# Two scan directions in lockstep, and one modulation product moved from VectorE to TensorE

## The chip, the cores and the metric

The kernel runs on one core of a Trainium2 chip. The metric is device time in microseconds for one execution of the whole program, and the median over several runs is compared. The profile is one further execution.

## The reference

A backbone of two layers over 1024 latent tokens of width 1024, with a prefix of 256 context tokens. Layer 0 mixes tokens with RWKV-7 scans in two directions, layer 1 with Fourier transforms; each is followed by a squared-ReLU MLP. Shift, scale and gate of every sub-layer come from a product of SiLU(c) with `mod_w`. Cut to what matters here:

```python
sh1, sc1, ga1, sh2, sc2, ga2 = jnp.split((silu_c @ mod_w[i] + mod_b[i])[:, None, :], N_MOD, axis=-1)
...
def step(s, inp):
    w_t, k_t, v_t, a_t, b_t = inp[:5]
    sa = jnp.einsum('bhvk,bhk->bhv', s, a_t)
    s = s * w_t[:, :, None, :] + sa[..., None] * b_t[:, :, None, :] + v_t[..., None] * k_t[:, :, None, :]
    y = jnp.einsum('bhvk,bhk->bhv', s, inp[5]) if with_out else None
...
for d in range(N_DIRS):
    rev = d == 1
    yc, s_ctx = _wkv_scan(st_c.get('r'), vh_c, *st_c['dirs'][d], s0, rev)
    yl, _ = _wkv_scan(st_l['r'], vh_l, *st_l['dirs'][d], s_ctx, rev)
    y_lat.append(yl)
```

There are 16 heads of 64 channels. The state of a head is a 64 by 64 matrix, and the latent scan starts from the state that the context scan of the same direction leaves.

## The kernel before

**Order of work.** Every operation is entered in a plan with an engine, a planned duration, the data it reads and writes, and for TensorE a load. `Plan.emit` then writes out an order for each engine: at each turn it takes the operation that can start first by its own model of times, and among equals the one with the longest tail of work behind it. On the chip each engine works through its list strictly in that order, and waits where data isn't there. The model also guesses the TensorE clock from planned loads, and puts dummy products on the identity matrix (L1814) where TensorE would otherwise stand still. A `flex` operation can go to one of several engines; the plan chooses.

**Stages.** `projections` computes keys, values, decays and so on and writes the scan's factors to DRAM. `scan` then takes 20 steps of 64 tokens: four of context (i = 0 to 3), sixteen latent. `rest` reads the scan's outputs back, gates and projects them, and runs the first MLP, the Fourier layer and the second MLP with products split in three.

**One scan step** (`scan_step`) handles 64 tokens of both directions d = 0, 1. Channels lie in eight tiles of 128, each of two heads (hh = 0, 1).

- Loads on SP: `bk` (512 KB a direction) and the `a`, `r` rows into `L`, later the values into `sv`.
- Scores: four TensorE operations (L945) into PSUM, spread by ScalarE (L954, L958) into `mab` and by VectorE, masked, into `L` (L961) and `l2` (L966).
- `bk` is turned by TensorE (L975, one operation of 16 transposes a direction, 64 rows by 128 columns of the array each) and copied to `bkt` (L979).
- `scan_invert` inverts the triangular blocks of both directions at once: transposes and small recursive products on VectorE (L1094 to L1138), then two TensorE operations on 32*32 tiles of the array, `h_mm` (L1145) and `t_mm` (L1156), 64 products each.
- The state that comes in is multiplied by the decay: two passes of 64 rows on VectorE into `sv` (L1001), one of 128 rows on GpSimd into `st` (L1004).
- For each direction in turn, a chain: `x_mm` (L1019), a ScalarE copy of half the rows (L1026), `u_mm` (L1031, 32*32 tiles), two ScalarE copies to `sv` (L1036), `o_mm` (L1044, 32*32 tiles), copy, `u_mm`, copies, then `s_mm` (L1056) and the new state (L1062). In latent steps `y_mm` (L1072, L1076) makes the output, which is copied (L1082) and stored.

A product of fp32 operands leaves two TensorE records in the trace, a transpose one. `sv` has a ring of three tiles, which the two directions take in turn.

**Modulation in the scan.** The first layer's four vectors that are needed after the scan (`mod_w[0][:, 2D:]`) are made beside it. `k_mwt` holds the weights transposed. From step 3 on, each of sixteen steps loads four pieces of 128 by 512 (L885, 256 KB each, ring `mw` of four), and VectorE multiplies each with a row of SiLU(c) and sums along it (L886). `mod_sum` adds the halves and the bias. The second layer's vectors are made in the same way during the first MLP (`modvecs`).

Of the kernel before, what the change touches and what calls it, by code (L numbers as in the profile page):

```python
# [12 lines left out]
AF = mybir.ActivationFunctionType  # L13
ALU = mybir.AluOpType
# [66 lines left out]
class Plan:  # L81
# [245 lines left out]
class Kernel:  # L327
# [449 lines left out]
    def factor(self, kt, low, d, c, k, k_k, kk, kkk, rr):  # L777
# [37 lines left out]
        self.flex_tt(n, bk[:, :ng, 0], gv(ta), p1[:, :ng], ALU.mult, [kta, kp1], [(kbk, 0)])  # L815
# [19 lines left out]
    def scan(self):  # L835
# [10 lines left out]
        for j, hp in enumerate(R["hp"]):  # L846
            plan.add("dve", 0.6, lambda hp=hp: nc.vector.tensor_copy(hp, self.cst[:, 0:32].rearrange("p (e c) -> p e c", e=1).broadcast_to(
                [P, 16, 32])), [self.kcst], [("hp", j)])
        self.state = {}
        for i in range(NCH):  # L850
            self.plan.step = i
            self.scan_step(i)
            if i == 3:
                past = plan.gate([("indt", 0), ("rts", 0), ("rts", 1)])
            if i in (3, 11):
                w, kw = slot("mw")
                self.silu_row(i // 8, lambda w=w: w, kw, [past, self.at])
            if 3 <= i < 19:
                for j in range(4):
                    w, kw = slot("mw")  # L860
                    self.mod_part(0, 16 + (i - 3) % 8 * 4 + j, (i - 3) // 8, lambda w=w: w, kw, [self.at])
            if i >= 11 and i < 19:
                self.mod_sum(0, 16 + (i - 11) * 4)
# [16 lines left out]
    def mod_part(self, layer, j, h, w, kw, after=()):  # L880

        nc = self.nc
        row = (j - 16 if layer == 0 else 32 + j) * P
        src = self.i["k_mwt"][row : row + P, h * 512 : h * 512 + 512]
        self.plan.add("q", 0.8, lambda: nc.sync.dma_start(w(), src), (), [kw], after=after, hold=0.7)  # L885
        self.plan.add("dve", 0.76, lambda: nc.vector.scalar_tensor_tensor(  # L886
            w(), w(), 1.0, self.silr, ALU.mult, ALU.mult,
            accum_out=self.macc[:, layer, h, j : j + 1]), ["silr"], [kw, ("macc", layer, h, j)])
# [11 lines left out]
    def scan_step(self, i):  # L900
# [3 lines left out]
        R0 = [slice(hh * 64, hh * 64 + 32) for hh in range(2)]  # L904
        R1 = [slice(hh * 64 + 32, hh * 64 + 64) for hh in range(2)]
# [24 lines left out]
        for d in range(2):  # L930
# [5 lines left out]
            for h4 in range(2):  # L936
# [13 lines left out]
                for hh, B in enumerate(BB):  # L950
# [3 lines left out]
                    plan.add("act", 0.38, lambda B=B, hh=hh, ys=ys: nc.scalar.activation(  # L954
                        mab[R0[hh], :, ys].rearrange("p w q t -> p q w t"),
                        B.tile[R0[hh]].rearrange("p (q w t) -> p q w t", q=4, w=4)[:, :, 0:2], AF.Copy, scale=-0.5),
                        [B], [(kM, d, hh, h4, 0)], B)
                    plan.add("act", 0.28, lambda bv=bv, hh=hh, ys=ys: nc.scalar.activation(  # L958
                        mab[R1[hh], 0, ys], bv()[R1[hh], :, 32:C], AF.Copy, scale=-0.5),
# [10 lines left out]
            BB = [self.plan.bank(range(4)) for _ in range(2)]  # L970

            def trs(BB=BB, bk=bk):
                for q in range(8):
                    for hh, rs in enumerate(HR):
                        nc.tensor.transpose(BB[hh].tile[:, q * C : (q + 1) * C], bk[rs, q, :], self.ident[rs, rs])  # L975

            plan.add("pe", 1.1, trs, [kb], [*BB, (kt_, 0), (kt_, 1)], load=0.5)
            for hh, B in enumerate(BB):
                plan.add("act", 0.68, lambda B=B, bkt=bkt, hh=hh: nc.scalar.activation(  # L979
                    bkt[:, hh].rearrange("p x t -> p (x t)"), B.tile, AF.Copy, scale=self.sgn[:, hh : hh + 1]),  # L980
                    [B, self.ksgn], [(kt_, hh)], B)
        tt, kT = self.scan_invert(mab, kM)

        for d in range(2):
# [12 lines left out]
            else:  # L997
                t, kt0, pcs = self.state[d]
                for hh in range(2):
                    rs = HR[hh]  # L1000
                    plan.add(("dve", "dve")[hh], 0.78, lambda rs=rs, hh=hh, d=d, t=t, sv=sv: (nc.vector, nc.vector)[hh].tensor_tensor(  # L1001
                        sv[rs, hh], t[rs], self.pcs[rs, d, :, i - 1 : i].broadcast_to([64, 8, C]), ALU.mult),
                        [kt0, *pcs], [(kv, "s0", hh), (kv, "s1", hh)])
                plan.add("pool", 1.22, lambda d=d, t=t, st=st: nc.gpsimd.tensor_tensor(  # L1004
                    st, t, self.pcs[:, d, :, i - 1 : i].broadcast_to([P, 8, C]), ALU.mult), [kt0, *pcs], [ks])
        for d in range(2):
            E = S[d]
            L, kL, sv, kv = E["L"], E["kL"], E["sv"], E["kv"]
            lall = [(kL, "a", 0), (kL, "a", 1)] + [(kL, "k", hh, h4) for hh in range(2) for h4 in range(2)]
            vall = [(kv, z, hh) for z in ("s0", "s1", "v") for hh in range(2)]  # L1010

            B, U = self.plan.bank(range(5,8)), self.plan.bank(range(5,8))
            quarter = [[slice(64 * z + 32 * hh, 64 * z + 32 * hh + 32) for hh in range(2)] for z in range(2)]

            def x_mm(B=B, L=L, sv=sv):
                for q in range(8):
                    for z in range(2):
                        for hh in range(2):
                            nc.tensor.matmul(B.tile[quarter[z][hh], q * C : (q + 1) * C], L[hh][:, q, 32 * z : 32 * z + 32],  # L1019
                                             sv[:, hh, q, :], start=z == 0 or q == 0, stop=z == 0)  # L1020

            self.at = plan.add("pe", 1.1, x_mm, lall + vall, [(B, 0), (B, 1)], B, load=0.78)
            for z, rows in enumerate((R0, R1)):
                half = slice(64 * z, 64 * z + 64)
                xs, kx = slot("xs")
                plan.add("act", 0.58, lambda B=B, xs=xs, half=half: nc.scalar.copy(xs[half], B.tile[half]), [(B, z)], [kx], B)  # L1026

                def u_mm(xs=xs, rows=rows, d=d, U=U, at=quarter[z]):
                    for q in range(8):
                        for hh in range(2):  # L1030
                            nc.tensor.matmul(U.tile[rows[hh], q * C : (q + 1) * C], tt[at[hh], d * 8 + q, :],  # L1031
                                             xs[at[hh], q * C : (q + 1) * C], start=True, stop=True)

                plan.add("pe", 1.08, u_mm, [kx, kT], [(U, z)], U, load=0.4)
                for hh in range(2):
                    plan.add("act", 0.58, lambda sv=sv, hh=hh, rows=rows, U=U: nc.scalar.copy(  # L1036
                        sv[rows[hh], hh].rearrange("p q c -> p (q c)"), U.tile[rows[hh]]), [(U, z)], [(kv, f"s{z}", hh)], U)
                if z:
                    continue

                def o_mm(B=B, sv=sv, d=d):
                    for q in range(8):
                        for hh in range(2):
                            nc.tensor.matmul(B.tile[quarter[1][hh], q * C : (q + 1) * C], mab[R0[hh], 1, d * 8 + q, :],  # L1044
                                             sv[R0[hh], hh, q, :], start=False, stop=q == 7)

                plan.add("pe", 1.08, o_mm, [(kv, "s0", 0), (kv, "s0", 1)] + [(kM, d, hh, h4, 0) for hh in range(2) for h4 in range(2)],
                         [(B, 1)], B, load=0.4)
# [15 lines left out]
            if lat:  # L1064
# [4 lines left out]
                def y_mm(B=Y, L=L, l2=l2, sv=sv, st=E["st"]):  # L1069
                    for q in range(8):  # L1070
                        for hh in range(2):
                            nc.tensor.matmul(B.tile[HR[hh], q * C : (q + 1) * C], L[hh][HR[hh], q, C:], st[HR[hh], q, :],  # L1072
                                             start=q == 0, stop=False)
                    for q in range(8):
                        for hh in range(2):
# [3 lines left out]
                plan.add("pe", 2.1, y_mm, vall + [E["ks"], (kL, "a", 0), (kL, "a", 1)]  # L1079
                         + [(k2, hh, h4) for hh in range(2) for h4 in range(2)], [Y], Y, load=0.85)  # L1080
# [5 lines left out]
    def scan_invert(self, mab, kM):  # L1086
# [23 lines left out]
        plan.add("dve", 1.5, four, [km], [kx, kta])  # L1110

        def double(n):

            for o in range(0, 16, 2 * n):
# [4 lines left out]
                def mul(o=o, ta=ta, pa=pa, z=z):  # L1119
                    p = at(ta, 0, [(n * n, n), (n, n), (1, n)])  # L1120
                    nc.vector.tensor_tensor(p, at(m, o + z, [(16, n), (0, n), (1, n)]), at(x, o, [(0, n), (1, n), (16, n)]), ALU.mult)
                    nc.vector.tensor_reduce(at(pa, 0, [(n, n), (1, n)]), p, AX.X, ALU.add)
                    nc.vector.tensor_tensor(p, at(x, o + z + n, [(16, n), (0, n), (1, n)]), at(pa, 0, [(0, n), (1, n), (n, n)]), ALU.mult)
                    nc.vector.tensor_reduce(at(x, o + z, [(16, n), (1, n)]), p, AX.X, ALU.add)

# [800 lines left out]
```

## Time and profile before

| what | value |
|---|---|
| median of 3 runs | 3099.05 us (3092.76 to 3102.13) |
| the profiled execution, its own time | 3100.86 us |
| span of the profile | 3099.1 us |
| mean granted TensorE clock | 0.93 |
| clock from 600 to 700 us, 1000 to 1100 us, 1600 to 1800 us | 0.71, 0.76, 1.00 |
| VectorE busy from 600 to 1300 us | 448.71 of 700 us |

Times in the profile are microseconds from the first instruction, single instructions are in ns where a row says so. A row of the timeline gives the start, the length from the first start to the last end, engine, line and operation, output and inputs, the tile of the array ("32*32": rows and columns used), and the count. A tile's letters stand for its place: `ps` for PSUM, the rest for places in SBUF. "issue" means that the engine waited for nothing that the profile shows. The granted clock is a share of full speed.

### The profile page before, as it was taken

Reading aid. Unit: us, or ns where it says so; the run is one execution under the profiler, and the core shown is the slowest. Engines: PE = TensorE matmul, PEld = TensorE weight load, DVE = VectorE, ACT = ScalarE, POOL = GpSimd, SP = SyncE. Lnnn points to the kernel's source line nnn. Section 1 sums busy time; section 2 is a strip of 40 time slices with the busy share of each in tenths; the row PEclk is TensorE's granted clock in tenths of the full one; section 3 lists DMA queues with packets and bytes.
Section 4 is the critical chain, followed back from the end, with each engine's and each line's share of the span. In section 5 each row is a group of like instructions: output and inputs, shape, how many; then the busy total and the mean of one; then the engine's idle time right before and its main releaser. Section 6 shows DMA issues by size and latency. Waiting matters only on the chain.

```text
span 3099.1 us, 65486 instructions
## 1 busy us (share of the span) xinstructions
PE 2905.6 (94%) x27884; PEld 2258.6 (73%) x27884; DVE 1902.2 (61%) x3316; ACT 998.6 (32%) x1943; POOL 535.9 (17%) x449
## 2 busy tenths in 40 slices
PE   9999989988878888799999999999899999999998
PEld 5443446477777777789878888888798788888887
DVE  5397785457666666687566556545877544554456
ACT  4363554245444555443211211111322111111121
POOL 2163452201001000111111001100331110111010
PEclk9999999967777877799999999999989999999999
DMA  9266476623344444553132323211031111111111
GB/s 276 86 182 174 136 194 177 160 66 100 107 128 124 134 117 120 158 186 102 58 109 92 96 89 107 70 48 47 8 120 42 52 47 38 55 48 48 41 45 55
DMA packets 297299, 313.03 MB, mean 101 GB/s; under 512 B 81024, under 2 KB 212224, under 8 KB 297008
## 3 DMA queue, kind: packets, MB, share of 16 engines
q1 hardware_dynamic: 295648, 304.01, 33.1%
q8 instruction: 219, 3.59, 0.5%
q0 software_dynamic: 1360, 4.84, 0.5%
q14 instruction: 72, 0.59, 0.1%
HBM read 246.38 MB, written 62.39 MB: 100 GB/s over the span
## 4 chain that ended last, share of the span: by engine, by line
PE 71%; DVE 10%; DMA 6%; issue 3%; ACT 2%; POOL 0%; SPq 0%; DVEq 0%; ACTq 0%; POOLq 0%
PE ps L364 16%; PE ps L366 16%; PE ps L365 16%; PE ps L617 4%; DMA sW<-in_k_mwt_dram 3%; PE ps L620 3%; PE ps L1031 2%; PE ps L945 2%; PE ps L1056 1%; PE ps L1044 1%; PE ps L1019 1%; PE ps L1072 1%; PE ps L1076 1%; DVE bU L456 1%; PE ps L1156 1%
## 5 line engine op out<-in xcount | busy, mean ns | idle before, releaser
L364 PE MATMUL ps<-rU,rU 128*128 128x512 f32 (+3 forms) x2632 | 979.0, 372 | 9.8 <-DVE rX L1509 8.0
L366 PE MATMUL ps<-rU,rU 128*128 128x512 f32 (+3 forms) x2632 | 974.9, 370 | 6.5 <-DVE rU L1239 3.7
L365 PE MATMUL ps<-rU,rU 128*128 128x512 f32 (+3 forms) x2632 | 974.6, 370 | 0.0
L364 PEld LDWEIGHTS ps<-rU,rU 128*128 128x128 f32 x2632 | 500.5, 190 | 105.1 <-DVE rX L1509 9.1
L366 PEld LDWEIGHTS ps<-rU,rU 128*128 128x128 f32 x2632 | 500.6, 190 | 98.0 <-DVE rU L1239 5.2
L365 PEld LDWEIGHTS ps<-rU,rU 128*128 128x128 f32 x2632 | 500.6, 190 | 89.5
L1509 DVE SCALAR_TENSOR_TENSOR rX<-ps,mods,rX 128x512 f32<-128x512 f32 (+1 forms) x528 | 375.6, 730 | 122.3 <-PE ps L366 120.5
L1239 POOL TENSOR_TENSOR rU<-rW,rU 128x512 fp32r<-128x512 f32 x73 | 117.2, 1611 | 1018.8 <-PE ps L366 521.7
L1488 ACT ACTIVATE rS<-ps 128x512 f32<-128x512 f32 x122 | 73.1, 599 | 680.9 <-PE ps L366 680.2
L620 PE MATMUL ps<-bU,bU 128*128 128x512 f32 (+1 forms) x544 | 237.5, 573 | 2.6 <-ACT bS L423 1.9
L423 ACT CAST rU<-rW 128x512 fp32r<-128x512 f32 x160 | 96.3, 616 | 346.8 <-PE ps L366 251.3
L423 DVE CAST rU<-rW 128x512 fp32r<-128x512 f32 x116 | 56.8, 500 | 221.0 <-PE ps L365 210.1
L423 DVE CAST rU<-rS 128x512 fp32r<-128x512 f32 (+1 forms) x99 | 46.9, 479 | 229.5 <-ACT rS L1491 203.4
L1239 DVE TENSOR_TENSOR rU<-rW,rU 128x512 fp32r<-128x512 f32 x201 | 175.5, 893 | 19.7 <-ACT rU L423 19.3
L620 PEld LDWEIGHTS ps<-bU,bU 128*128 128x128 f32 x544 | 100.2, 193 | 109.1 <-issue 98.2
L617 PE MATMUL ps<-bU,bU 128*128 128x512 f32 x304 | 141.7, 607 | 0.0
L945 PE MATMUL ps<-sU,sX 64*128 64x128 f32 (+1 forms) x1280 | 125.5, 353 | 16.8 <-DVE sU L961 7.8
L945 PEld LDWEIGHTS ps<-sU,sX 64*128 64x128 f32 x1280 | 111.9, 255 | 25.2 <-issue 11.7
L961 DVE TENSOR_TENSOR sU<-ps,sW 64x256 f32<-64x256 f32 x160 | 67.5, 422 | 85.7 <-ACT sX L954 44.8
L1239 POOL TENSOR_TENSOR rU<-rS,rU 128x512 fp32r<-128x512 f32 x39 | 60.7, 1559 | 280.8 <-ACT rU L423 125.9
L1036 ACT COPY sU<-ps 32x512 f32<-32x512 f32 x160 | 92.3, 577 | 43.4 <-PE ps L1031 40.2
L617 PEld LDWEIGHTS ps<-bU,bU 128*128 128x128 f32 x304 | 56.6, 192 | 61.6 <-issue 57.8
(268 smaller groups left out, 3899.2 us busy)
## 6 DMA issues: line engine op xcount, KB each, us to landing
rW<-in_mlp_w_dram SPq DMA_DIRECT2D x256, 256.0 KB
rW<-in_k_mwt_dram SPq DMA_DIRECT2D x96, 256.0 KB
sX<-s_bk SPq DMA_DIRECT2D x40, 512.0 KB
s_ar<-bU SPq DMA_DIRECT2D x32, 512.0 KB
sU<-s_ar SPq DMA_DIRECT2D x64, 256.0 KB
sW<-in_k_mwt_dram SPq DMA_DIRECT2D x64, 256.0 KB
bU<-in_rk_wk_dram SPq DMA_DIRECT2D x48, 256.0 KB
bU<-in_rk_wv_dram SPq DMA_DIRECT2D x48, 256.0 KB
```

The source lines that it names most:

```text
L364: nc.tensor.matmul(out, w[0], x[0], start=start, stop=False)
L365: nc.tensor.matmul(out, w[0], x[1], start=False, stop=False)
L366: nc.tensor.matmul(out, w[1], x[0], start=False, stop=stop)
L423: self.nc.scalar.copy(out, src) if e == "act" else self.engines[e].tensor_copy(out, src)
L617: fn = lambda B=B, x=x, w=w, ms=ms, kt=kt: nc.tensor.matmul(B.tile, x[:, ms], w, start=kt == 0, stop=kt == KT - 1)
L620: fn = lambda B=B, x=x, w=w, ms=ms, kt=kt, n=n: nc.tensor.matmul(B.tile[:, :n], w[:, ms], x[:, :n], start=kt == 0, stop=kt == KT - 1)
L945: nc.tensor.matmul(BB[hh].tile[:, j * P : j * P + nr], bk[HR[hh], q, :], L[hh][HR[hh], q, :nr], start=True, stop=True)
L961: plan.add("dve", 0.41, lambda bv=bv, ro=ro, hh=hh, q4=q4, d=d, L=L: nc.vector.tensor_tensor(L[hh][ro, q4, 0:C], bv()[ro, :, 0:C], self.ma ...
L1036: plan.add("act", 0.58, lambda sv=sv, hh=hh, rows=rows, U=U: nc.scalar.copy(sv[rows[hh], hh].rearrange("p q c -> p (q c)"), U.tile[rows[hh ...
L1239: plan.flex({"dve": n / 960 + 0.07, "pool": n / 440 + 0.08}, lambda e: self.engines[e].tensor_tensor(out(1), src(), f32(out(0)), ALU.subtr ...
L1488: plan.flex({"act": 0.53, "dve": 0.6}, lambda e, B=B, s=s: nc.scalar.activation(s.tile[:, :512], B.tile, AF.Relu) if e == "act" else nc.ve ...
L1509: plan.add("dve", n / 960 + 0.12, lambda B=B, m=m, n=n, xs=xs: nc.vector.scalar_tensor_tensor(xs(), B.tile[:, :n], self.mod(layer, 5, m), ...
```

## The change

The diff does several things, all in the scan:

- The two directions share `u_mm` and `o_mm`. The rows of a direction's two halves are swapped for d = 1 (`RZ`), so that four 32*32 tiles of the array serve both directions and both heads in one operation. `x_mm` writes both directions' results into two shared banks, one copy of 128 rows takes the place of two of 64, and the eight copies to `sv` may go to ScalarE or VectorE.
- The transposes of `bk` leave their own operation and are issued inside `h_mm` (direction 0) and `t_mm` (direction 1): after the four products of each y, one transpose. Each of the two is planned as two halves.
- The decay of the state is one VectorE pass of 128 rows into `st`, copied from there to `sv`; GpSimd has no part in it.
- `y_mm` is planned as two operations, `r_mm` and `y_mm`.
- The inversion's VectorE steps are planned one by one, and two of them read and write their scratch tile in another order.
- Modulation of the first layer: `k_mw1` holds the weights in their own order. `mod_block` loads four pieces a step, multiplies each on TensorE with a 32-column tile of SiLU(c) (one strip of the array each), copies the bank to SBUF on ScalarE, turns it with four products against `sel`, and copies eight columns out on VectorE. The rows of SiLU(c) (`silu_row`) are no longer made in the scan.

The core of the diff:

```diff
+                for q in range(8):
+                    for d, hh in four:
+                        rs = RZ[z][d][hh]
+                        nc.tensor.matmul(U.tile[rs, q * C : (q + 1) * C], tt[rs, d * 8 + q, :], xs[rs, q * C : (q + 1) * C],
+                                         start=True, stop=True)
...
+                plan.add("dve", 0.76, lambda d=d, t=t, st=st: nc.vector.tensor_tensor(
+                    st, t, self.pcs[:, d, :, i - 1 : i].broadcast_to([P, 8, C]), ALU.mult), [kt0, *pcs], [ks])
                 for hh in range(2):
-                    rs = HR[hh]
-                    plan.add(("dve", "dve")[hh], 0.78, ...
-                plan.add("pool", 1.22, ...
+                    plan.flex({"act": 0.58, "dve": 0.45}, lambda e, hh=hh, sv=sv, st=st: self.copy_on(e, sv[HR[hh], hh], st[HR[hh]]),
...
+        def turn(d, y):
+            nc.tensor.transpose(TB[d][y % 2].tile[:, y // 2 * C : (y // 2 + 1) * C], S[d]["bk"][HR[y % 2], y // 2, :], self.ident[HR[y % 2], HR[y % 2]])
...
-        def h_mm():
-            for y in range(16):
+        def h_mm(w):
+            for y in range(8 * w, 8 * w + 8):
                 for q in Q:
                     nc.tensor.matmul(H.tile[q, y * 16 : y * 16 + 16], mab[q, 0, y, :], xt[q, y, 0:16], start=True, stop=True)
+                turn(0, y)
...
+        def t_mm(w):
+            for y in range(8 * w, 8 * w + 8):
+                for q in Q:
+                    nc.tensor.matmul(T.tile[q, y * 32 : y * 32 + 32], hp[q, y, :], xd[q, y, :], start=True, stop=True)
+                turn(1, y)
...
+    def mod_block(self, j, h):
+        W = [slot("mw") for _ in range(4)]
+        for k, (w, kw) in enumerate(W):
+            ...
+            plan.add("q", 0.8, lambda w=w, src=src: nc.sync.dma_start(w, src), (), [kw], after=[self.at], hold=0.7)
+        def products():
+            for k, (w, _) in enumerate(W):
+                nc.tensor.matmul(B.tile[32 * k : 32 * k + 32], silc[:, 4 * h + k], w, start=True, stop=True)
+        plan.add("pe", 0.6, products, [kw for _, kw in W] + [ksil], [B], B)
+        plan.add("act", 0.58, lambda: nc.scalar.copy(e, B.tile), [B], [ke], B)
+        def turn():
+            for x in range(4):
+                nc.tensor.matmul(V.tile[:, 2 * x : 2 * x + 2], e[:, x * P : (x + 1) * P], self.sel, start=True, stop=True)
+        plan.add("pe", 0.5, turn, [ke], [V], V, load=0.0)
```

The planned durations in these lines are the scheduler's, not measurements. The rest of the kernel is built as before, in the order that the plan then gives.

More of the change, by code (lines that the diff above doesn't have):

```diff
@@ L903, in scan_step @@
         nr = P if lat else C
[L904 to L905 removed]
+        RZ = [[[slice(hh * 64 + 32 * (d ^ z), hh * 64 + 32 * (d ^ z) + 32) for hh in range(2)] for d in range(2)] for z in range(2)]
         HR = [slice(hh * 64, hh * 64 + 64) for hh in range(2)]
@@ L969, in scan_step @@
                             [B, self.kmask], [(k2, hh, h4)], B)
[L970 to L982, printed above, removed]
+        tt, kT = self.scan_invert(mab, kM, S)
         for d in range(2):
@@ L1018, in x_mm @@
                         for hh in range(2):
-                            nc.tensor.matmul(B.tile[quarter[z][hh], q * C : (q + 1) * C], L[hh][:, q, 32 * z : 32 * z + 32],
+                            nc.tensor.matmul(XB[z].tile[RZ[z][d][hh], q * C : (q + 1) * C], L[hh][:, q, 32 * z : 32 * z + 32],
                                              sv[:, hh, q, :], start=z == 0 or q == 0, stop=z == 0)
[L1022 to L1048, printed above, removed]
@@ L1049, in scan_step @@
+        for d in range(2):
+            E = S[d]
+            L, kL, sv, kv, vall = E["L"], E["kL"], E["sv"], E["kv"], vkeys[d]
             if i < NCH - 1:
@@ L1150, in scan_invert @@
             hp[:, :, 0:16], H.tile[:, :256].rearrange("p (y s) -> p y s", y=16), hi,
[L1151 to L1158 removed]
+            self.cst[:, 0:16].rearrange("p (e c) -> p e c", e=1).broadcast_to([P, 16, 16]), ALU.mult, ALU.add), [(H, 0), (H, 1), self.kcst], [khp])
+        turned(0)
+        def t_mm(w):
[3 more added lines that the diff above has]
+                turn(1, y)
+        for w in range(2):
+            plan.add("pe", 1.3, lambda w=w: t_mm(w), [khp, kxd, S[1]["kb"]], [(T, w), *[(X, w) for X in TB[1]]], load=0.55)
+        turned(1)
         tt, kT = slot("tt")
[L1160 removed]
+        plan.add("act", 0.58, lambda: nc.scalar.copy(tt.rearrange("p y t -> p (y t)"), T.tile), [(T, 0), (T, 1)], [kT])
         return tt, kT
```

134 lines of the change are left out of this document (82 added, 52 removed), and 4 rows, old and new, of the table SCAN_RINGS.

## The prediction, as put on record before the result

> **What bounds the kernel now.** I read the page first, then the granted clock by stretch, the busy time of a whole number of scan steps, the groups of that stretch, the waits, and last the timeline of TensorE, one record at a time. The page:
>
> ```profile
> span 3099.1 us, 65486 instructions
> PE 2905.6 (94%) x27884; PEld 2258.6 (73%) x27884; DVE 1902.2 (61%) x3316; ACT 998.6 (32%) x1943; POOL 535.9 (17%) x449
> PEclk9999999967777877799999999999989999999999
> ```
>
> TensorE is busy nearly throughout, but its granted clock falls to 0.7 in slices 9 to 18, about 640 to 1340 us: the scan, the only place that this change rewrites. After it TensorE is full (the split MLP products), so a microsecond more or less in the scan moves the end by about one.
>
> The transpose that opens an inversion (L1094) runs once a step. From the one at 844.22 to the one at 1263.76 there are twelve steps:
>
> ```profile
> 844.22 1.02 DVE L1094 STREAM_TRANSPOSE sS<-sX 128x512 f32<-128x512 f32 x1
> 1263.76 1.02 DVE L1094 STREAM_TRANSPOSE sS<-sX 128x512 f32<-128x512 f32 x1
> 844.22:1263.76 419.54, 345.00 (x10370) 315.34 (x10370) 286.47 (x643) 207.14 (x444) 40.35 (x38) 0.78 0.42 123
> L1094 DVE STREAM_TRANSPOSE sS<-sX 128x512 f32<-128x512 f32 x12 | 12.3, 1026 | 0.0
> ```
>
> A step takes 419.54/12 = 34.96 us: TensorE busy 28.75, VectorE 23.9, ScalarE 17.3, clock 0.78. TensorE stands still 6.2 us a step, and these waits show for what:
>
> ```profile
> PE ps L1145 <- issue: 18.7, 8, 3.7
> PE ps L975 <- DVE sU L966: 10.1, 3, 3.6
> PE ps L1156 <- issue: 6.2, 4, 2.2
> L886 DVE SCALAR_TENSOR_TENSOR sW<-sW,sF 128x512 f32<-128x512 f32 x49 | 32.5, 683 | 49.4 <-DMA sW<-in_k_mwt_dram 49.4
> L1001 DVE TENSOR_TENSOR sU<-sU,pcs 64x512 f32<-64x512 f32 x48 | 47.4, 988 | 1.2
> 861.43 7.06 SPq L885 DMA_DIRECT2D sW<-in_k_mwt_dram  x4
> 876.03 0.69 DVE L886 SCALAR_TENSOR_TENSOR sW<-sW,sF 128x512 f32<-128x512 f32 x1 [10.78 <-DMA sW<-in_k_mwt_dram]
> ```
>
> VectorE stops 49.4/12 = 4.1 us a step for the modulation weights, which here land 14.6 us after their issue; part of it returns as TensorE's waits on L966. So TensorE bounds a step, with a stalled VectorE second. TensorE must be priced piece by piece. Its timeline at the full clock, then at half:
>
> ```profile
> 1131.79 1.08 PE L1031 MATMUL ps<-sU,sW 32*32 32x64 f32 x32
> 1132.80 0.71 PE L975 MATMUL ps<-ident,sX 64*128 64x64 f32 x16
> 1133.45 1.10 PE L1019 MATMUL ps<-sU,sU 128*32 128x64 f32 x64
> 1134.48 1.15 PE L1056 MATMUL ps<-sU,sU 128*64 128x64 f32 x32
> 1135.56 1.15 PE L1072 MATMUL ps<-sU,sU 64*64 64x64 f32 x32
> 1185.21 1.29 PE L1145 MATMUL ps<-sU,sX 32*32 32x16 f32 x124
> 1186.43 2.12 PE L945 MATMUL ps<-sU,sX 64*128 64x128 f32 x32
> 1188.48 0.30 PE L1044 MATMUL ps<-sU,sX 32*32 32x64 f32 x4
> 1097.11 2.08 PE L1156 MATMUL ps<-sU,sU 32*32 32x32 f32 x128
> 1099.00 1.19 PE L1031 MATMUL ps<-sU,sS 32*32 32x64 f32 x30
> 1147.96 3.79 PE L945 MATMUL ps<-sU,sX 64*128 64x128 f32 x32
> 1160.97 1.91 PE L1044 MATMUL ps<-sU,sX 32*32 32x64 f32 x30 [0.18 <-ACT sU L1036]
> 1162.81 1.97 PE L1072 MATMUL ps<-sU,sU 64*64 64x64 f32 x32
> 1164.71 0.59 PE L1076 MATMUL ps<-sU,sU 128*64 128x64 f32 x6
> ```
>
> From start to next start, full/half clock, for one step: four score products (L945) 4.1/7.4; two blocks of transposes (L975) 1.3/2.3; the two small blocks of the inversion (L1145, L1156) 2.6/3.8; two x (L1019) 2.1/3.7; four u and two o (L1031, L1044) 6.1/11.0; two s (L1056) 2.2/3.8; the four halves of y (L1072, L1076) 4.3/7.6. Where a half-clock row is missing (x, transposes) I took 1.8 times the full one, the ratio of L945. Sum 22.7/39.6. The measured 28.75 lies 0.36 of the way, and I keep that share.
>
> **What a change of shape costs.** The starts show more: between blocks of different tile shape there is a hole that no row calls idle.
>
> ```profile
> L975 PE MATMUL ps<-ident,sX x16: 221/223/273, 1132.8 to 1133.3; 64*128 64x64 f32 x16
> L1044 PE MATMUL ps<-sU,sX x32: 214/214/309, 1126.1 to 1127.1; 32*32 32x64 f32 x32
> 1125.41 0.71 PE L975 MATMUL ps<-ident,sX 64*128 64x64 f32 x16
> 1126.05 1.36 PE L1044 MATMUL ps<-sU,sX 32*32 32x64 f32 x32
> 1143.94 0.22 PE L1044 MATMUL ps<-sU,sX 32*32 32x64 f32 x2
> 1143.95 0.22 PE L1145 MATMUL ps<-sU,sX 32*32 32x16 f32 x7
> ```
>
> A transpose record lasts 0.22, so the last of the 16 began at 1125.41 + 0.71 - 0.22 = 1125.90, and the 32*32 block began 0.15 later, against 0.49/15 = 0.03 between two transposes. L1145 (0.18 a record) ends in the same way: last start 1186.32, next shape 1186.43, 0.11. At half clock L1044 (0.31) to L1072 gives 1162.57 to 1162.81, 0.24. Blocks of one shape mix with no hole: L1044 and L1145 above start 0.01 apart. The Trainium skill says as much (TensorEngine Tiling (Array Packing), Key Properties: "Changing tiling mode (not just tile) drains the TensorE"); it gives no figure, and the trace's 0.11 to 0.15 us is used.
>
> **The change part by part.**
>
> *The transposes move into the inversion's blocks.* This is the dear one. Each of 32 rounds a step is now eight records of 32*32 (four products, two records each), one 64*128 transpose, then 32*32 again: 64 changes of shape a step where two blocks of transposes had four. A round at full clock: eight records at 1.22/124 = 0.08, 0.11 out, 0.15 back, 0.34; with 32 columns (t) a little more, 0.36. Sixteen of each: 11.2 us. At half: 0.12 (1.89/128 x 8, from L1156 above) + 0.14 (my estimate between 0.11 and 0.24) + 0.24 = 0.50, 16.0 us. Before, the same work was 3.9/6.1. So +7.3/+9.9 us a step. Bounds: 0, if a change inside a block cost nothing, and +9.9. I take the rows' value, since every change of shape that I followed has the hole.
>
> *Both directions in one u and one o.* Six blocks of 32 records become three of 64 on four tiles. Nearest row: L1019, 64 records on four strips, 1.03 (half, 1.87): 3.1/5.6, saving 3.0/5.4. One of the Trainium skill's rules would take that away (TensorE: Matmul & The Clock Gate, "Wait — 56ns, not 53.3ns?": start-to-start never below about 25 ns): 64 records would be 1.6, the saving 1.2 instead of 3.0, and the time about 36 us later. The trace disagrees for records on different tiles: 124 of L1145 in 1.22 us are 10 ns each.
>
> *x, s, r and y* keep their counts. y's split only frees the first half from waiting for l2.
>
> *Modulation on TensorE.* Nearest rows:
>
> ```profile
> 17.02 1.07 PE L524 MATMUL ps<-aX,aX 128*32 128x256 f32 x16
> 18.02 0.71 PE L1814 MATMUL ps<-ident 128*128 128x128 f32 x4
> 18.58 0.61 PE L534 MATMUL ps<-sel,aX 128*128 128x2 f32 x4
> L1036 ACT COPY sU<-ps 32x512 f32<-32x512 f32 x97 | 56.0, 577 | 22.9 <-PE ps L1031 20.9
> ```
>
> Sixteen records of 256 columns took 1.00; a block has eight of 512, so 1.0/1.8. Turning the row back: two products took four records in 0.61, so four about 1.0/1.5. Together +2.0/+3.3 a step in the 16 steps that have it, plus one ScalarE copy (0.58, as L1036) and a tiny VectorE copy. VectorE loses four passes (32.5/12 = 2.7 us) and the 4.1 us stop. The four 256 KB loads a step stay on SP; there they can hold up the next step's loads only when their ring is still being read. But the products wait for all four, and behind them on TensorE stands everything: the stop changes engines. It is covered if TensorE reaches the products more than some 14 us after the issue; if not, the bound is the present 4.1 us a step, 66 in all.
>
> *State decay.* The two half-height passes on VectorE (L1001, 47.4/12 = 3.95 us a step) and one on GpSimd become one full pass a direction, 0.69 (a full pass of L886) to 0.99 each, and four copies shared by ScalarE and VectorE; u's eight copies may now go to VectorE too. VectorE ends at 21 us or less, ScalarE near 17: neither bounds. The shorter inversion chain on VectorE is hidden for the same reason; if TensorE were no bound it would be worth under 1 us.
>
> *The sum.* TensorE: 4.1 + 11.2 + 2.1 + 3.1 + 2.2 + 4.3 + 2.0 = 29.0 at full clock, 7.4 + 16.0 + 3.7 + 5.6 + 3.8 + 7.6 + 3.3 = 47.4 at half; at 0.36 of the way, 35.6 against 28.75. Idle time: of the 6.2 us now, the issue waits inside L1145 and L1156 (24.9/12 = 2.1) should go, since those blocks now draw instructions at under half the pace, and part of the waits on VectorE; I leave 3.5. Step 39.1, +4.1. Sixteen latent steps: +66. Four context steps have no y, and only the last has a modulation block: +7.3 - 3.0, less 2.1 of issue, is about +2.5 each, +10. Together +76, rounded +80. The profiled run took 3100.86, 1.8 more than its span and the same again over the median of 3099.05: I predict 3180. With the share of half clock between 0.2 and 0.6 (the inversion now is a long stretch of tiny products, which argues for more) TensorE is at 32.7 to 40.0, and with 2.5 to 4.0 us idle this case gives 3110 to 3270.
>
> **The rivals.**
>
> *Faster: the change of shape is not paid inside a block.* Place: the 32 rounds; price: 7.3/9.9 us a step; it decides if a round takes under about 0.2 us. Then TensorE needs 21.7/37.5, 27.4 at the same share; with 3 us idle the step is 30.4, 16 x 4.6 + 4 x 4 = 90 less: 3010. For it: no row shows a single 32*32 to 64*128 round trip inside one block. Against it: the hole is there each time a block of one shape follows another. 24 in 100.
>
> *No change.* TensorE's added work fills its 6.2 us of idle time and the clock rises with it: step 35, 3100. Against it: 35.6 busy alone is more. 7 in 100.
>
> *Slower still: the ring of sv.*
>
> ```profile
> 821.47 6.94 DMA sU<-s_v
> PE ps L1019 <- DMA sU<-s_v: 0.2, 1, 0.2
> ```
>
> Three tiles serve two directions. In lockstep the second direction's tile for the next step is the first one's of this step, free only after its y; a load of s_v stands 6.94 us on the chain that ended last. From s to the next x: s 1.08, state 0.69, decay 0.69, copy 0.58, x 1.03 and handovers, some 4.5; y lies 2.2 behind s, so up to 6.9 + 2.2 - 4.5 = 4.6 us a step are exposed where no score product is ready to fill it. Today 0.2 us in twelve steps. On top of the forecast: 3260. 13 in 100.
>
> **How the numbers follow.** Forecast 56 in 100. Differences within 0.3%, 9 us, cannot be told from none here. Faster 0.24 (the first rival), same 0.07, slower 0.69 (forecast and ring). The range reaches into the faster rival and to the ring's time: 2995 to 3270, with about one in ten left out on either side.
>
> **What would show it.** Right: the step, from one L1094 to the next, near 39 us; each of the two inversion blocks 5 to 8 us on TensorE with 0.1 to 0.25 us on either side of each transpose; VectorE's wait for modulation weights gone; clock in the scan at or below 0.78. Wrong: rounds near 0.15 us; a step near 30; or TensorE waiting for loads where it now waits for issue.

## The result, and the profile after

The changed kernel took 3231.84 us in the median of four runs (3223.85 to 3239.69), the kernel before 3099.2 (3092.76 to 3102.13): ratio 1.0431, with a 95% interval of 1.0397 to 1.0464, 133 us slower. The forecast was 3180, in a range of 2995 to 3270.

Lines moved: the transpose that opens an inversion is L1114 now (L1094 before), the turning of `bk` L1168 (L975), `h_mm` L1180 (L1145), `t_mm` L1194 (L1156), the scores L972 (L945), `x_mm` L1030 (L1019), `u_mm` L1045 (L1031), `o_mm` L1059 (L1044), the dummy products L1855 (L1814). New are the modulation's products L875 and its turns L883. The page, as far as it answers to the rows shown of before:

```profile
span 3225.7 us, 66273 instructions
PE 3105.4 (96%) x28424; PEld 2356.0 (73%) x28424; DVE 1842.2 (57%) x3233; ACT 982.9 (30%) x1914; POOL 495.0 (15%) x421
PEclk9999999967787777889999999999989999999999
```

TensorE has 200 us more of busy time, VectorE 60 less. Twelve scan steps again, from the first inversion shown to the thirteenth, with the stretch of the four context steps (first inversion to fifth) above it. Columns: length; TensorE, its weight loads, VectorE, ScalarE, GpSimd busy; clock; DMA share; GB/s.

```profile
646.90:774.90 128.00, 121.79 (x2244) 101.73 (x2234) 62.36 (x147) 46.01 (x108) 2.68 (x5) 0.66 0.19 56
897.04:1379.10 482.06, 462.82 (x10808) 368.82 (x10807) 244.31 (x574) 201.27 (x431) 8.91 (x19) 0.79 0.35 106
```

A step takes 482.06/12 = 40.17 us: TensorE 38.57 busy and 1.6 idle (before 28.75 and 6.2), at a clock of 0.79 (before 0.78). The difference of the two spans, 126.6 us, lies here: context steps 36.7 (128.0 against 91.3), fifteen latent steps 76.2 (40.28 against 35.20 each), what follows the last inversion 11.3, what precedes the first 2.4.

The groups of TensorE in those twelve steps, and three groups of before:

```profile
L1168 PE MATMUL ps<-ident,sX 64*128 64x64 f32 x380 | 123.1, 324 | 0.0
L1194 PE MATMUL ps<-sU,sU 32*32 32x32 f32 x1536 | 59.5, 232 | 2.0 <-DVE sU L1186 1.6 <-issue 0.4
L1180 PE MATMUL ps<-sU,sX 32*32 32x16 f32 x1496 | 50.9, 200 | 1.8 <-issue 1.8
L1059 PE MATMUL ps<-sU,sX 32*32 32x64 f32 x768 | 21.2, 217 | 7.9 <-DVE sU L423 4.5 <-ACT sU L423 3.1 <-issue 0.2
L1855 PE MATMUL ps<-ident 128*128 128x128 f32 x100 | 17.9, 314 | 1.5 <-issue 1.2 <-ACT sX L985 0.3
```

```profile
L975 PE MATMUL ps<-ident,sX 64*128 64x64 f32 x384 | 22.2, 269 | 10.3 <-DVE sU L966 10.1
L1156 PE MATMUL ps<-sU,sU 32*32 32x32 f32 x1536 | 20.2, 208 | 13.5 <-DVE sU L1149 7.3 <-issue 6.2
L1145 PE MATMUL ps<-sU,sX 32*32 32x16 f32 x1536 | 19.6, 185 | 18.7 <-issue 18.7
```

The same transposes and inversion products fill 233.5 us instead of 62.0, though one lasts only 8 to 20% longer. Before, the records of a block overlapped (384 transposes of 269 ns made 22.2 us); now each transpose stands alone (380 of 324 ns make the whole 123.1). From start to next start, where overlaps count once, a step's inversion with its transposes takes 14.95 us of TensorE, before 4.82. The waits for issue, 24.9 us on the two inversion lines before, are 2.2 now. The timeline shows why, at full clock and at half:

```profile
672.15 0.25 PE L1180 MATMUL ps<-sU,sX 32*32 32x16 f32 x8
672.33 0.27 PE L1168 MATMUL ps<-ident,sX 64*128 64x64 f32 x1
672.53 0.25 PE L1180 MATMUL ps<-sU,sX 32*32 32x16 f32 x8
676.46 0.30 PE L1180 MATMUL ps<-sU,sX 32*32 32x16 f32 x8
676.69 0.36 PE L1168 MATMUL ps<-ident,sX 64*128 64x64 f32 x1
676.99 0.30 PE L1180 MATMUL ps<-sU,sX 32*32 32x16 f32 x8
```

A round of eight records and one transpose takes 0.38 us at full clock (0.18 to the transpose, 0.20 back) and 0.53 at half (0.23 and 0.30). No row calls any of it idle.

The tile shape makes the hole, and not the alternation of transposes with products: where the last transpose is followed by scores, which have its shape, the scores start with it.

```profile
688.04 0.36 PE L1168 MATMUL ps<-ident,sX 64*128 64x64 f32 x1
688.04 2.07 PE L972 MATMUL ps<-sU,sX 64*128 64x64 f32 x16
```

The scan has eleven such places, and in all of them the scores start 2 to 3 ns after the transpose; 32*32 products start 0.19 to 0.30 us after it.

### The profile page after: what moved, and what is told of

Its sections match the earlier page's. It is cut to its first block, busy times and chain, and to the rows that moved or that the text cites. A ratio compares the mean times of both kernels' runs of the same rounds, so it can differ in the third digit from the quotient of the medians.

```text
span 3225.7 us, 66273 instructions
## 1 busy us (share of the span) xinstructions
PE 3105.4 (96%) x28424; PEld 2356.0 (73%) x28424; DVE 1842.2 (57%) x3233; ACT 982.9 (30%) x1914; POOL 495.0 (15%) x421
## 4 chain that ended last, share of the span: by engine, by line
PE 47%; DVE 3%; issue 1%; ACT 0%; POOL 0%; DMA 0%; DVEq 0%; ACTq 0%; POOLq 0%
PE ps L364 15%; PE ps L366 15%; PE ps L365 15%; DVE rU L1280 1%; DVE rU L423 0%; DVE rS L1649 0%; PE ps L1855 0%; PE ps L1446 0%; DVE rU L1481 0%; DVE rS L1476 0%; PE ps L1457 0%; DVE rS L1657 0%; DVE rX L1836 0%; DVE rS L1610 0%; DVE rU L1664 0%
## 5 line engine op out<-in xcount | busy, mean ns | idle before, releaser
L366 PE MATMUL ps<-rU,rU 128*128 128x512 f32 (+3 forms) x2632 | 975.4, 371 | 11.2 <-DVE rU L1280 8.4
L1168 PE MATMUL ps<-ident,sX 64*128 64x64 f32 x640 | 208.6, 326 | 0.0
L620 PEld LDWEIGHTS ps<-bU,bU 128*128 128x128 f32 x544 | 99.6, 191 | 105.8 <-issue 96.9
L433 POOL TENSOR_SCALAR sU<-sS,sS 128x256 f32<-128x256 f32 x28 | 13.5, 490 | 749.7 <-DVE sS L1147 719.1
L1168 PEld LDWEIGHTS ps<-ident,sX 64*128 64x128 f32 x640 | 102.6, 160 | 28.8 <-issue 0.2
L972 PE MATMUL ps<-sU,sX 64*128 64x128 f32 (+1 forms) x1280 | 111.3, 319 | 9.6 <-DVE sU L988 6.1
L1855 PE MATMUL ps<-ident 128*128 128x128 f32 x708 | 106.5, 308 | 8.8 <-DMA ident<-in_k_ident_dram 2.7
```

The source lines that it names most:

```text
L366: nc.tensor.matmul(out, w[1], x[0], start=False, stop=stop)
L620: fn = lambda B=B, x=x, w=w, ms=ms, kt=kt, n=n: nc.tensor.matmul(B.tile[:, :n], w[:, ms], x[:, :n], start=kt == 0, stop=kt == KT - 1)
L972: nc.tensor.matmul(BB[hh].tile[:, j * P : j * P + nr], bk[HR[hh], q, :], L[hh][HR[hh], q, :nr], start=True, stop=True)
L1168: nc.tensor.transpose(TB[d][y % 2].tile[:, y // 2 * C : (y // 2 + 1) * C], S[d]["bk"][HR[y % 2], y // 2, :], self.ident[HR[y % 2], HR[y % 2]])
L1855: self.plan.fill = lambda t: nc.tensor.matmul(t[:, :P], self.ident, self.ident, start=True, stop=True)
```

## The experiments

All were timed against the kernel before on the same chip. "Changes" counts how often the tile shape on TensorE changes in a scan step: 16.4 before, 78 after.

**1. The interleaving alone, in the kernel before.** The two blocks of transposes are taken out and each transpose is put behind the four products of its round; nothing else of the change is there, except that the two inversion blocks are planned in halves.

```diff
-            plan.add("pe", 1.1, trs, [kb], [*BB, (kt_, 0), (kt_, 1)], load=0.5)
+            for y in range(8 * w, 8 * w + 8):        # h_mm; t_mm in the same way
                 for q in Q: nc.tensor.matmul(H.tile[q, ...], mab[q, 0, y, :], xt[q, y, 0:16], ...)
+                turn(0, y)
...
```

> The kernel before the change with one part of it: the transposes inside the inversion's rounds. Directions one after the other, modulation on VectorE. Theory: 64 changes of shape cost 9 to 10 us of TensorE a step, the waits for instructions (5.5 us a step) shrink: 5 to 6 us a step more, and a stretch of dummies in the context steps: 3200 to 3235 us. That is, this part alone makes the whole loss. Rival (the loss needs the lockstep, where nothing else can fill TensorE): under 3150.

3207.62 us, ratio 1.0333 [1.0308, 1.0358]. Its twelve steps:

```profile
892.48:1353.54 461.06, 452.22 (x10418) 380.63 (x10417) 280.00 (x649) 207.00 (x445) 39.85 (x37) 0.78 0.38 115
```

38.42 us a step, TensorE busy 37.69. This part by itself makes 3.33 of the 4.31% lost, some 103 of 133 us: most of the loss and not, as expected, the whole.

**2. The change without the interleaving.** Transposes as operations of their own ahead of the inversion, as before; lockstep and modulation on TensorE stay. The two inversion blocks are whole again.

```diff
-                turn(0, y)
-                turn(1, y)
+            plan.add("pe", 1.1, trs, [kb], [*BB, (kt_, 0), (kt_, 1)], load=0.5)
...
```

> The changed kernel with the transposes as operations of their own, planned ahead of the inversion as before the change; lockstep and modulation on TensorE stay. With the eight together behind the rounds it was 3112 us, 35.3 us a step, TensorE idle 7.2 us a step for its instructions. Theory (TensorE is short of instructions: they come in blocks of 256, some 50 a us, and the lockstep saves time but no instruction): the step stays at 34 to 36 us; the four context steps lose their stretch of dummies and come down from 98 to about 91 us: 3095 to 3110 us. Rival (lockstep itself is a gain that only the holes hid): a step of 31 to 33 us, 3040 to 3070.

3081.77 us, ratio 0.9934 [0.9919, 0.9949]: 0.7% faster than the kernel before and 150 us less than the changed one. The time lies between the two expectations.

```profile
837.82:1240.44 402.62, 326.22 (x10532) 282.21 (x10519) 243.60 (x579) 199.94 (x431) 8.82 (x17) 0.85 0.44 129
```

A step is 33.55 us, TensorE 27.18 of it, and the four context steps are back to 85.5 us.

**3 and 4. The dose.** In the changed kernel, eight transposes behind eight rounds (3), or two behind two rounds (4). The same instructions, in another order.

```diff
-                turn(0, y)                                 # 3, and t_mm in the same way
+            for y in range(8 * w, 8 * w + 8):
+                turn(0, y)
-                turn(0, y)                                 # 4
+                if y % 2:
+                    turn(0, y - 1)
+                    turn(0, y)
```

> The changed kernel (3231.8 us) with one thing altered: in each of the four half blocks of the inversion the eight transposes stand behind the eight rounds of 32*32 products instead of one after each round. Same instructions, same plan, 8 changes of shape a step instead of 64. Theory (each change of tile shape leaves a hole on TensorE, and TensorE bounds the scan): a round took 0.38 us at full clock and 0.53 at half in the changed kernel; without the changes it is about 0.11 and 0.17, so 28 x 0.27 = 7.6 to 28 x 0.36 = 10.1 us a step less on TensorE, 20 steps: 150 to 200 us, of which some comes back as waits: 3050 to 3110 us, that is, about as before or faster. Rival 1 (the lockstep chain or its loads bound the scan, the inversion lies beside it): within 20 us of 3232. Rival 2 (the modulation on TensorE is the cost): also 3232.

> The changed kernel with the transposes two at a time, after every second round: 32 changes of shape a step instead of 64. Theory of the shape changes: 16 x 0.27 = 4.3 to 16 x 0.36 = 5.8 us a step less, 20 steps: 85 to 115 us, so 3115 to 3150 us; per change saved the same as in the run with all eight together. Rivals as there: within 20 us of 3232.

Grouped: 3112.13 us, 1.0044 [1.0022, 1.0066], 2 us above the range that the theory gave. In pairs: 3137.12, 1.0114 [1.0068, 1.0159]. The groups in twelve steps, first (3), then (4):

```profile
L1168 PE MATMUL ps<-ident,sX 64*128 64x64 f32 x376 | 26.2, 269 | 4.5 <-issue 4.4
L1195 PE MATMUL ps<-sU,sU 32*32 32x32 f32 x1536 | 23.8, 212 | 19.1 <-issue 18.7 <-DVE sU L1187 0.2
L1180 PE MATMUL ps<-sU,sX 32*32 32x16 f32 x1472 | 19.6, 183 | 12.8 <-issue 12.7
```

```profile
L1168 PE MATMUL ps<-ident,sX 64*128 64x64 f32 x378 | 59.8, 310 | 1.7 <-issue 1.7
L1196 PE MATMUL ps<-sU,sU 32*32 32x32 f32 x1536 | 37.7, 219 | 6.3 <-issue 4.5 <-DVE sU L1188 1.6
L1180 PE MATMUL ps<-sU,sX 32*32 32x16 f32 x1472 | 32.3, 192 | 4.0 <-issue 4.0
```

| | changes a step | inversion with transposes | TensorE idle | clock | step | time |
|---|---|---|---|---|---|---|
| changed | 78 | 14.95 us | 1.6 | 0.79 | 40.17 | 3231.8 |
| pairs | 46 | 8.65 | 3.8 | 0.83 | 36.04 | 3137.1 |
| grouped | 23 | 5.29 | 7.2 | 0.86 | 35.27 | 3112.1 |

From 23 to 78 changes the inversion grows by 9.66 us: 0.175 us a change, the lower clock of the changed kernel included. From pairs to grouped it falls by another 3.36, but the waits for issue, 2.2 us a step with pairs and 5.8 grouped, take back nearly all of it: as the holes go, something that they covered appears.

**5. Is that cover the supply of instructions?** The grouped kernel with half as many inversion products, each twice as wide (for odd y they use the neighbour's weights).

```diff
-            for y in range(8 * w, 8 * w + 8):
+            for y in range(8 * w, 8 * w + 8, 2):
                 for q in Q:
-                    nc.tensor.matmul(H.tile[q, y * 16 : y * 16 + 16], mab[q, 0, y, :], xt[q, y, 0:16], ...)
+                    nc.tensor.matmul(H.tile[q, y * 16 : y * 16 + 32], mab[q, 0, y, :], xt[q, y : y + 2, 0:16], ...)
```

> The run with the eight transposes together (3112 us), and the inversion's two blocks made of half as many products, each twice as wide: one weight tile for two neighbouring y, so half of the inversion's products use the wrong weights and the work on every second y is left out. 256 instructions a step fewer of some 1795, TensorE's busy time only about 1 us less. Theory (supply of instructions bounds the step): 256 at 50 a us are 5 us, of which 3 to 5 show, in 20 steps 60 to 100 us: 3010 to 3050. Rival (TensorE's busy time and its order bound): 1 us a step, 3085 to 3100.

3076.78 us, 0.9912 [0.9896, 0.9929]; between the two expectations. A step takes 33.2 us: busy time fell by 2.0, idle time only from 7.16 to 7.06. Most of the waits moved to another line, the scores. First the grouped kernel's waits in its twelve steps (total, times, longest), then this one's:

```profile
PE ps L972 <- issue: 21.0, 5, 5.7
PE ps L1195 <- issue: 18.7, 9, 3.4
PE ps L1180 <- issue: 12.7, 8, 3.2
```

```profile
PE ps L972 <- issue: 35.1, 6, 10.0
PE ps L875 <- DMA sW<-in_k_mw_dram: 12.9, 5, 8.0
```

Over all lines the waits for issue fell from 5.8 to 4.8 us a step, and waits for the modulation weights (12.9 us in twelve steps, before 5.1) took most of that place. So the supply theory fell in its size, 3 to 5 us a step; the little that it lost is in proportion to the instructions left out, and what the waits are is open.

**6. The dummy products.** None in the scan up to the last step.

```diff
-            op["fills"] = fills, blank
+            op["fills"] = 0 if op["step"] is not None and op["step"] < NCH - 1 else fills, blank
```

> The changed kernel without the dummy products on the identity that the plan puts into the scan (some 270 records between 620 and 1380 us against 38 before the change); the order is the same. Theory: the plan's TensorE runs ahead of the real one, so most dummies stand in no gap and cost their own time, 0.12 to 0.3 us a record: 25 to 50 us less, 3180 to 3207. Rival: they stand in true waits and hold the clock up: 3232 or some 10 us more.

3222.51 us, 1.0389 [1.0349, 1.0430]: 9 us less, not 25 to 50, and the two intervals overlap. The step is 39.73:

```profile
892.71:1369.45 476.74, 454.59 (x10713) 360.27 (x10715) 244.25 (x573) 201.18 (x431) 8.96 (x19) 0.77 0.36 108
```

Of 1.38 us of dummies a step, 0.44 came off. TensorE stands still only 0.25 us longer (1.85); its other products take 0.7 us longer, at a clock of 0.77 instead of 0.79. The context steps keep their 126.8 us.

**7, 8 and 9. The modulation.** 7 is the changed kernel with VectorE's passes; 8 the kernel before with the products on TensorE (one PSUM bank for products and turns, one tile of `td`); 9 is experiment 2 with VectorE's passes, so the lockstep with the smaller parts of the change (the state's decay, y in two operations, VectorE's steps in the inversion).

```diff
-            if 3 <= i < 19:                                # 7 and 9; 8 the other way round
-                self.mod_block(*divmod(i - 3, 2))
+            if 3 <= i < 19:
+                for j in range(4):
+                    w, kw = slot("mw")
+                    self.mod_part(0, 16 + (i - 3) % 8 * 4 + j, (i - 3) // 8, lambda w=w: w, kw, [self.at])
...
```

> The changed kernel with the first layer's modulation back in VectorE passes (transposed weights, rows of SiLU(c)); all else as changed. Theory (TensorE bounds the scan, VectorE has 12 us a step free): TensorE loses the products and turns, 2.45 us a step in 16 steps, VectorE takes 2.7 us and a wait for the load that its free time covers: about 40 us less, 3190 us. Rival 1 (the modulation is most of the loss): 3130 or less. Rival 2 (VectorE's stop for the load comes back onto the path): 3232 or more.

> The kernel before the change with the first layer's modulation on TensorE (the row is turned in the bank that the products used, one bank a block instead of two). Theory (instructions bound the step): 32 instructions a step more, VectorE's stop of 4.1 us goes but was not the bound: 3085 to 3115 us. Rival (VectorE's stop for the load bounded the step): 4 us in 16 steps, 3035 us. Second rival (TensorE's busy time bounds): 2.4 us in 16 steps more, 3138.

> The lockstep alone: transposes in operations of their own ahead of the inversion, and the first layer's modulation in VectorE passes as before. Theory (merged u and o save TensorE about 3 us a step, the modulation on TensorE costs it 1.2 to 2.5): 3055 to 3075 us, 10 to 25 less than with the products on TensorE (3081.8), a scan step of 32 to 33 us. Rival (VectorE's stop for the modulation weights and its four passes come back and cost what TensorE saves): 3080 to 3100, a step at 33.5 or above with TensorE waiting for VectorE.

7: 3212.63 us, 1.0362 [1.0322, 1.0402], 19 less than the changed kernel, half of what was expected. 8: 3161.26, 1.0184 [1.0156, 1.0213], a miss. Its trace shows two things: eleven steps of 35.7 us (the same eleven before: 34.7), and a last interval, from the nineteenth inversion to the twentieth, of 73.6 instead of 38.1. There the loads of the last step's `bk` stand on SP behind stores of outputs that were not ready:

```profile
1261.05 6.70 SPq L867 DMA_DIRECT2D sW<-in_k_mw_dram  x4
1284.24 0.49 SPq L935 DMA_DIRECT2D s_y<-sS  x1
1284.83 0.58 SPq L1252 DMA_DIRECT2D rW<-s_y  x1
1288.72 0.49 SPq L935 DMA_DIRECT2D s_y<-sS  x1
1290.06 2.75 SPq L935 DMA_DIRECT2D sX<-s_bk  x2
```

In the kernel before they were issued at 1230.38, ahead of its stores. So 36 of its 57 us (1.84%) are the written order of the last step, and the rest would be some 1.3 us for each of sixteen steps; the eleven steps of the trace show 1.0.

9: 3046.86 us, 0.9827 [0.9802, 0.9851], the best of all, 8 us below what the theory expected. Twelve steps:

```profile
828.20:1221.90 393.70, 307.33 (x10568) 279.81 (x10569) 265.91 (x667) 196.34 (x425) 7.91 (x16) 0.84 0.45 132
```

32.81 us a step, TensorE busy 25.61 against 27.18 with the products on it, while VectorE, with its passes back, is busy for 22.2 of 32.8 and makes TensorE wait 1.2 us a step:

```profile
PE ps L980 <- DVE sU L1001: 5.7, 4, 2.4
PE ps L1110 <- DVE sU L1100: 5.0, 2, 2.5
PE ps L1187 <- DVE sU L1180: 3.5, 1, 3.5
```

As far as one written order of each can tell, the lockstep with the smaller parts gains 54 us, and the products on TensorE take 35 of them back.

**10, 11 and 12. The ring of sv.** A fourth tile, taken from `l2`, in experiment 2 (10), in the changed kernel (12) and in the lockstep alone (11).

```diff
-    ("sv", (2, 8, C), *_u(12, 13, 14)), ("l2", (8, 2, C), *_u(15, 16, 17, 18, 19, 20)),
+    ("sv", (2, 8, C), *_u(12, 13, 14, 20)), ("l2", (8, 2, C), *_u(15, 16, 17, 18, 19)),
```

> Separate transposes, lockstep and products on TensorE, with a fourth tile in the ring of sv (taken from l2, which keeps five). Theory: in lockstep no wait for a load of s_v shows, so the ring is no cost: 3075 to 3090, as with three tiles (3081.8). Rival (the ring of three holds the loads back by way of the queue on SP): 3030 to 3065.

> The changed kernel with a fourth tile in the ring of sv (l2 keeps five). Theory (TensorE is busy for 38.6 of the 40.2 us of a step, so an earlier load of s_v has nothing to fill): 3215 to 3245 us, as the changed kernel (3231.8). Rival (the ring of three tiles is part of the loss, as the 26 us between three and four tiles with separate transposes say): 3190 to 3212.

> The lockstep alone (separate transposes, modulation on VectorE) with four tiles of sv. If the ring is a cost of its own, it comes off again: 3015 to 3032 us. If the 26 us came from the order that the planner happens to write with every edit, there is no reason for them to return: 3040 to 3065.

10: 3055.86 us, 0.9857 [0.9834, 0.9881], 26 less than with three tiles: the rival's time. 12: 3291.53, 1.0635 [1.0608, 1.0661], 60 more than the changed kernel. 11: 3052.55, 0.9850 [0.9826, 0.9875], the same as with three tiles within the scatter. One edit, three signs: a ring that cost time would have given its gain in each. What else moves is the order that the planner writes out, for every engine, from the scan on. In 12 the inversions come at uneven distances, TensorE's clock falls to 0.73, and the loads of modulation weights now stop it, for 8.2 us in twelve steps:

```profile
899.20:1431.90 532.70, 493.55 (x10852) 391.56 (x10848) 253.01 (x591) 201.09 (x434) 8.69 (x15) 0.73 0.33 99
```

```profile
PE ps L875 <- DMA sW<-in_k_mw_dram: 8.2, 3, 5.4
```

Whether `l2`'s lost tile has a part in the 60 us was not tried. That the order makes the differences is the likely reading and was not shown. For all the runs here it follows that one small edit can move this kernel by 26 or 60 us beside what it was made for: the 19 us of 7 prove nothing by themselves, and the 9 us of 6, where the order is the same, lie within the scatter. The interleaving is above this: adding it cost 103 us, taking it away gave 120 (grouped) and 150 (experiment 2), and half of its changes 95.

## Why the prediction was right

Slower was right, and 3231.8 lies in the range; the forecast of 3180 itself was 52 us short. The clock in the scan, forecast at or below 0.78, was 0.79.

**The change of shape inside a block** was the deciding step, and it held: 0.38 us a round at full clock and 0.53 at half against 0.34 to 0.36 and 0.50. The faster rival needed under 0.2 and is out by the timeline; experiments 1 to 4 put the loss there by adding it, removing it and grading it. The "estimate between 0.11 and 0.24" for the way out at half clock, 0.14, measures 0.14 from the last record's start to the transpose. The term was a little small all the same: 14.95 us a step of inversion and transposes, where 11.2 and 16.0 at the share of 0.36 give 12.9. The way back was the short piece: 0.20 at full clock and 0.30 at half where 0.15 and 0.24 were taken, 1.6 to 1.9 us in 32 rounds.

**The other pieces of TensorE** came out as summed: scores 4.92, x 2.94, u 2.35, o 1.72, s 2.44, the two halves of y 2.82 and 2.62, products 1.63, turns 0.82; together 22.3 against the 22.7 that the forecast of 35.6 leaves them. In it, u and o fell from 7.81 to 4.07, a saving of 3.7 (3.0 to 5.4 predicted). By the floor of about 25 ns from start to start in the Trainium skill (TensorE: Matmul & The Clock Gate, "Wait — 56ns, not 53.3ns?") the 192 records of u and o would take an estimated 4.8 us or more. The trace disagrees again: they took 4.07, and the 128 of u 2.35, 18 ns apart.

**The idle time left** was put at 3.5 and is 1.6. The waits for issue in the inversion went as said. That VectorE's stop for the weights would go was right as well, and so was that it would not come back on TensorE; the loads' row among its weight loads' waits, in the changed kernel:

```profile
PEld ps L875 <- DMA sW<-in_k_mw_dram: 4.2, 10, 0.6
```

Experiment 12, where the same loads stop TensorE, shows that another edit can take this cover away.

**What the sum lacked.** Dummy products: eight a step, 1.38 us, where there was almost none before (0.04). They stand in the busy time, so 1.9 us less of idle time and 1.4 more of dummies are nearly one thing; experiment 6 gives 9 us for all of them. In sum, 39.1 + 2.05 (inversion) - 0.4 (other pieces) + 1.4 (dummies) - 1.9 (idle) = 40.2: the latent steps missed by 1.0 us each, some 15 in all. That it was not more is in part that these errors have different signs.

**The step that failed is the context steps**: "about +2.5 each, +10" was +36.7 in all. This is 27 of the 52 us that the forecast was short. The price of the holes held: the grouped kernel, with its transposes in the same operations, has 98.5 us for this stretch, so the holes make 29.5, 7.4 a step. What was taken off against them did not come: 3.0 for u and o and 2.1 of issue, some 20 in four steps, as if TensorE bound these steps too. Experiment 2 saves 5.8, with TensorE busy for 69.3 of 85.5 us. The stretch of the grouped kernel, then of experiment 2:

```profile
645.00:743.50 98.50, 87.16 (x2247) 79.30 (x2241) 62.09 (x146) 46.00 (x108) 2.96 (x5) 0.75 0.25 72
647.40:732.90 85.50, 69.33 (x1982) 63.68 (x1973) 57.98 (x138) 43.32 (x106) 1.93 (x4) 0.63 0.24 71
```

The 13.0 between these two were not in the sum at all: the transposes had a second use in their old place, where they filled the wait for the first inversions. Of the changed kernel, then of the one before:

```profile
651.25 6.01 PE L972 MATMUL ps<-sU,sX 64*128 64x64 f32 x48
657.56 14.65 PE L1855 MATMUL ps<-ident 128*128 128x128 f32 x108 [0.31 <-DVE sU L988]
```

```profile
650.51 3.68 PE L945 MATMUL ps<-sU,sX 64*128 64x64 f32 x32
655.34 1.12 PE L975 MATMUL ps<-ident,sX 64*128 64x64 f32 x15 [1.05 <-ACT sX L958]
657.72 1.12 PE L975 MATMUL ps<-ident,sX 64*128 64x64 f32 x15 [0.21 <-ACT sU L979]
```

Tied to the inversion, they come only when it does, and dummies fill the wait. That the tie makes the whole 13.0 was not shown: experiment 2 also has another order. With the interleaving alone the stretch is 132.4 us, 41 more than before. After the last inversion, the sum had +4.1 for the sixteenth latent step, and +11.3 came; in the grouped kernel it is +0.7, so most of it is the holes again.

**No change and the ring.** TensorE's work did not fit into its idle time: it grew by 9.8 us a step, all but 1.6 of the idle time was filled, and the step still grew by 5.2; the clock rose only from 0.78 to 0.79. A ring of `sv` as a cost is not supported: in the scan of the changed kernel TensorE waits for no load of `s_v`, and a fourth tile made it slower.

## What to carry to other kernels

Before small products are mixed on TensorE, compare the tile shapes: each change cost 0.10 to 0.30 us here, 0.175 on the mean, in time that a profile counts as busy, and is seen only in the distance from the start of one row to the start of the next. A block that looks free to move may be what fills another wait, so ask what stands in its old place. And where a planner writes the order, a difference of some tens of microseconds from one edit needs a second edit with another order before it is called a cause: here one ring size gave -26, +6 and +60.

## What the runs showed that was not expected

When the holes are closed TensorE waits for issue, 5.8 us a step in the grouped kernel and 4.9 in experiment 2 (before 3.2), with nothing that the profile shows as its releaser. In the grouped kernel the timeline has such gaps in the middle of a block:

```profile
1107.49 0.63 PE L1180 MATMUL ps<-sU,sX 32*32 32x16 f32 x53
1110.75 0.39 PE L1180 MATMUL ps<-sU,sX 32*32 32x16 f32 x11 [2.64 <-issue]
1143.04 0.31 PE L1195 MATMUL ps<-sU,sU 32*32 32x32 f32 x10
1146.28 0.67 PE L1195 MATMUL ps<-sU,sU 32*32 32x32 f32 x54 [2.93 <-issue]
```

In each of the two a packet of 16 KB on the queue q8, kind instruction, was under way; the DMA view of the first gap counts it:

```profile
q8 instruction: 1, 0.02, 2.3%
```

Worked out from the records of that queue: of 30 gaps over 0.8 us in those twelve steps, 22 end 1.0 to 1.6 us after such a packet has landed; before, 20 of 33 do, where chance would give 12%. Of those among them that the profile puts down to issue, it is 22 of 27, and before 19 of 19. About seven packets come a step, never closer than 3.35 us. That TensorE now and then outruns its instructions fits this, and dense small products are where it would. Experiment 5 took away a seventh of the packets (72 instead of 85) and a sixth of the waits for issue, but hardly any idle time, so it is a reading and not shown.
